# Neighbourhood-attention scores of two heads made together, with the low-part products on half of TensorE's rows each

## The chip, the cores and the metric

The kernel runs on one core of one Trainium2 chip. The metric is the device time of one execution in microseconds (us), as the median of several runs. One further execution was taken by the hardware profiler, and its trace is what is read here.

## What is computed

One layer of a hybrid transformer over 1024 latent tokens (16 rows of a 64-wide grid) with 256 context tokens, width 1024. One input projection feeds a windowed attention (mixer A) and a neighbourhood attention (mixer B), each of 8 query heads of 64 elements. Their outputs are normalised, projected and followed by a SwiGLU feed-forward part (FFN). The change touches the scores of mixer B alone:

```python
def _neighbourhood_latent(q, k, v, k_ctx, v_ctx, rpb):
    ...
    s_loc = jnp.einsum('bnqhd,bnjhd->bnhqj', qb, kg).astype(jnp.float32) * scale + bias
    s_loc = jnp.where(jnp.asarray(mask)[:, None], s_loc, -jnp.inf)
    s_ctx = jnp.einsum('bnqhd,bjhd->bnhqj', qb, k_ctx).astype(jnp.float32) * scale
    p = jax.nn.softmax(jnp.concatenate([s_loc, s_ctx], axis=-1), axis=-1)
    ...
    o = (jnp.einsum('bnhqj,bnjhd->bnqhd', p_loc, vg)
         + jnp.einsum('bnhqj,bjhd->bnqhd', p_ctx, v_ctx))
```

## The kernel before, in words

Products that need more precision than TensorE's one-pass type `F32R` gives are made from two parts: `split` (L117) writes a high part on ScalarE (L119) and the rest, the low part, on VectorE (L122). A head has 64 elements, so the two parts of a head together fill the 128 rows of TensorE.

**Keys of mixer B.** The loop at L357 makes the keys of 128 tokens at a time. `khl` (L366) holds, for each of 8 heads, the high part and then the low part, 64 elements each. It is stored to `kb_d`. `b_kv` (L548) loads it back and transposes it on TensorE, so that `KT[h]` has the head's high part in rows 0 to 63 and its low part in rows 64 to 127, with 1024 local keys and 256 context keys as columns.

**Queries of mixer B.** A step u of the main loop (L893, sixteen of them) is one strip of 16 grid columns (`C`, four) and one pair of heads (`hp_`, four). `b_q` (L568) loads the queries of its two halves (`R`, 8 grid rows each) and two heads, transposes them, and splits them into `QTh` and `QTl`. The store (L535) wrote each query twice, so `QTh[:, j]` has the high part in rows 0 to 63 and again in rows 64 to 127, and `QTl[:, j]` has the low part twice.

**Scores.** `b_front` (L598) calls `scores` (L448) for each half and head, 64 times in all. One call takes a PSUM tile `s` of 1024 columns (the tag has two buffers) and issues four matmuls over all 128 rows at L455: `QTh` against the 256 context keys and the 384 local keys, then `QTl` against the same. So a score is (q high + q low) times (k high + k low). Right behind it VectorE adds the bias and finds the row maximum (`P`, `nm`, L617), ScalarE takes the exponential (L619), and after the four calls of a step GpSimd scales by the reciprocal sum (L625). A `yield` after each call lets `run` put one piece of the step before between two calls.

**The piece of the step before** is `b_back` (L627): four transposes of `P` (L639), a copy out of PSUM (L642 on VectorE, L644 on ScalarE), and products with the values (L652, L656). Those last have 64 columns of weights and write 64 PSUM partitions: head 0 the lower 64, head 1 the upper 64. Their operands are plain f32, and the trace has two instructions for each such `T.matmul`.

**What else runs in these steps.** The output projection of finished tiles: `out_proj` (L809), with TensorE lines L818 to L820 in `F32R`, 512 columns each; and, from u = 10 on, the transposes of `out_b2` (L880). Keys of later head pairs are transposed at L559, queries at L576.

**Order.** The program's order is not the source's. A planner (`schedule_with_timeline_sim=True`, L1385) simulates the kernel when it is built and fixes each engine's order; every engine then executes its list in order. Waits between engines and for buffers are put in by the framework.

Of the kernel before, what the change touches and what calls it, by code (L numbers as in the profile page):

```python
# [7 lines left out]
F32 = mybir.dt.float32  # L8
# [10 lines left out]
HD = 64  # L19
# [37 lines left out]
def f(ap):  # L57
    return ap.bitcast(F32)


def block(tc, d, out, dbg=()):
    nc = tc.nc
    V, S, G, T = nc.vector, nc.scalar, nc.gpsimd, nc.tensor
    load = nc.sync.dma_start

    def pool(name, bufs=1, space=None, side=None):
        kw = {}
        if space is not None:
            kw["space"] = space
        if side is not None:  # L70
            kw["side"] = side
        return tc.alloc_tile_pool(name=name, bufs=bufs, reuse_waits="tile", **kw)
# [44 lines left out]
    def split(hi, lo, src, hi_eng, lo_eng):  # L117
        if hi_eng is S:
            S.activation(hi, src, AF.Copy)  # L119
        else:  # L120
            hi_eng.tensor_copy(hi, src)
        lo_eng.tensor_tensor(lo, src, f(hi), op=ALU.subtract)  # L122
# [118 lines left out]
    def wsplit(wp, nr, nw, c0, n):  # L241
        return [wsplit_k(wp, nr, nw, c0, n, k, V if k % 2 else G) for k in range(8)]
# [11 lines left out]
    def gemm(m, ws, n, tag):  # L254
        pg = gtile(tag)
        for k in range(8):
            gemm_k(pg, m, k, ws[k], n)
        return pg
# [29 lines left out]
    def rope_tables(ipc):  # L288
        ropet = ipc.tile([128, 4, 8, HD], F32, name="ropet")
        load(ropet, d["rope"])  # L290
        gain = ipc.tile([128, 2, HD], F32, name="gain")
        for j, nm in enumerate(("qn_a", "kn_a")):
            load(gain[:, j], d[nm].to_broadcast([128, HD]))
        gsw = ip.tile([128, 512], F32, name="gsw", tag="w1")[:, :2 * HD].rearrange(
            "p (g e) -> p g e", g=2)
        gv = gain[:, 0:2].rearrange("p g (b s q) -> p (g b) s q", b=2, s=2)
        gw = gsw.rearrange("p g (b s q) -> p (g b) s q", b=2, s=2)
        V.tensor_copy(gw[:, :, 0], gv[:, :, 1])
        V.tensor_copy(gw[:, :, 1], gv[:, :, 0])
        for j in range(2):  # L300
            V.tensor_tensor(ropet[:, 2 * j], ropet[:, 2 * j],
                            gain[:, j:j + 1].to_broadcast([128, 8, HD]), op=ALU.mult)
            V.tensor_tensor(ropet[:, 2 * j + 1], ropet[:, 2 * j + 1],
                            gsw[:, j:j + 1].to_broadcast([128, 8, HD]), op=ALU.mult)
        tb.update(ropet=ropet, gain=gain)
# [3 lines left out]
    def store(dst, src, lag=2):  # L309

        waiting.append((dst, src))
        while len(waiting) > lag:
            load(*waiting.pop(0))
# [9 lines left out]
    def headnorm(ps, nh, p):  # L323
        n = nh * HD
        qc = p.tile([128, 512], F32, name="qc", tag="w2")
        S.activation(qc[:, :n], ps, AF.Copy)  # L326
        sq = p.tile([128, 512], F32, name="hsq", tag="w1")
        S.activation(sq[:, :n], qc[:, :n], AF.Square)
        ss = p.tile([128, 32], F32, name="hss")
        V.tensor_reduce(ss[:, :nh], sq[:, :n].rearrange("p (h e) -> p h e", e=HD), axis=AX.X,  # L330
                        op=ALU.add)
        r = rstd_of(p, ss[:, :nh], HD, nh, "hr")
        q3 = qc[:, :n].rearrange("p (h e) -> p h e", e=HD)
        V.tensor_tensor(q3, q3, r.unsqueeze(2).to_broadcast([128, nh, HD]), op=ALU.mult)
        return qc
# [21 lines left out]
    for m in range(10):  # L357
        if m == MV:
            wsv = wsplit(wl, RL, 8, 1792, 512)
        if m == MV + 2:  # L360
            rope_tables(ipc)
        pg = pgs[m] if m < NF else gemm(m, ws, 512, "i")
        qn = headnorm(pg, 8, ip)
        q3 = qn.rearrange("p (h e) -> p h e", e=HD)
        (V if m % 2 else G).tensor_tensor(q3, q3, gkb[:, 0:1].to_broadcast([128, 8, HD]), op=ALU.mult)
        khl = wi.tile([128, 8, 2, HD], F32R, name="khl", bufs=KLB)  # L366
        split(khl[:, :, 0], khl[:, :, 1], q3, S, V)
        store(kb_d[m * 128:(m + 1) * 128], f(khl), LAG)

    def v_b(m, ws, tag):  # L370
# [9 lines left out]
    for m in (8, 9, 0, 1, 2, 3, 4, 5, 6, 7):  # L380
        pg = gemm(m, ws, 256, "i")
        S.activation(Va[:, m].rearrange("p g e -> p (g e)"), pg[:, 128:256], AF.Copy)
        qn = headnorm(pg[:, :128], 2, ip)
# [36 lines left out]
    for m in range(8):  # L420
        pg = gemm(m, ws, 512, "i")
        qn = headnorm(pg, 8, ip)
# [9 lines left out]
    psA = pool("psA", space=PSUM)  # L432
# [15 lines left out]
    def scores(segs, lh, ll):  # L448
        s = psA.tile([128, 1024], F32, name="s", tag="s", bufs=2)
        for n_, l in enumerate((lh, ll)):  # L450
            for o, rhs, n in segs:
                ov = s[:, o:o + n]
                if len(rhs.shape) == 3:
                    ov = ov.rearrange("p (r c) -> p r c", c=rhs.shape[2])
                T.matmul(ov, l, rhs, start=n_ == 0, stop=n_ == 1)  # L455
        return s

    def geo(i):
        b0, b1 = max(i - 1, 0), min(i + 1, 7)
        nl = (b1 - b0 + 1) * 128  # L460
        if i == 7:
            return b0, nl, 512, 256, 256, 0, [8, 9] + list(range(b0, b1 + 1))
        return b0, nl, 512 - nl, 512, 512 - nl, 256 + 384 - nl, list(range(b0, b1 + 1)) + [8, 9]
# [9 lines left out]
    def a_front(i, g, Ps, QT):  # L473
        QTh, QTl = QT
        b0, nl, lo_o, cx_o, s0, m0, blocks = geo(i)
        n = nl + CTX
        nm = at.tile([128, 64], F32, name="nm", bufs=3)[:, :4]
        den = at.tile([128, 64], F32, name="den", bufs=3)[:, :4]
        for h in range(4):
            hh = 4 * g + h  # L480
            s = scores([(lo_o, KTa[:, g, b0 * 128:b0 * 128 + nl], nl),
                        (cx_o, KTa[:, g, SEQ:SEQ + CTX], CTX)],
                       QTh[:, h * 128:(h + 1) * 128], QTl[:, h * 128:(h + 1) * 128])
            P = at.tile([128, 640], F32, name="P", bufs=10)
            V.tensor_tensor_reduce(P[:, :n], s[:, s0:s0 + n], mska[:, m0:m0 + n], -1.0,  # L485
                                   nsink[:, hh:hh + 1], ALU.add, ALU.min, nm[:, h:h + 1])
            S.activation(P[:, :n], P[:, :n], AF.Exp, scale=-1.0, bias=nm[:, h:h + 1],  # L487
                         accum_out=den[:, h:h + 1])
            Ps.append(P)
            yield  # L490
        es = at.tile([128, 128], F32, name="es", bufs=3)[:, :4]
        V.tensor_tensor(es, nm, sink[:, 4 * g:4 * g + 4], op=ALU.add)
        S.activation(es, es, AF.Exp)
        V.tensor_tensor(den, den, es, op=ALU.add)
        V.reciprocal(den, den)  # L495
        for h in range(4):
            G.tensor_scalar(Ps[h][:, :n], Ps[h][:, :n], den[:, h:h + 1], 1.0, ALU.mult, ALU.mult)  # L497
# [100 lines left out]
    def b_front(hp_, C, Ps, QT, bias):  # L598
        QTh, QTl = QT
        KT = kvs[hp_]  # L600
        nm = atb.tile([128, 64], F32, name="nm", bufs=3)[:, :4]
        den = atb.tile([128, 64], F32, name="den", bufs=3)[:, :4]
        for R in range(2):
            r0 = 4 * R
            for h in range(2):
                j = 2 * R + h
                kl = KT[h][:, :SEQ].rearrange("p (r c) -> p r c", c=64)[
                    :, r0:r0 + 12, C0S[C]:C0S[C] + 32]
                kc = KT[h][:, SEQ:]
                if R == 0:  # L610
                    s = scores([(256, kc, 256), (512, kl, 384)], QTh[:, j], QTl[:, j])
                    s0, m0 = 256, 384
                else:
                    s = scores([(128, kl, 384), (512, kc, 256)], QTh[:, j], QTl[:, j])
                    s0, m0 = 128, 0
                P = atb.tile([128, 640], F32, name="P", bufs=PBB)
                V.tensor_tensor_reduce(P, s[:, s0:s0 + 640], bias[h][:, m0:m0 + 640], -1.0,  # L617
                                       3.0e38, ALU.add, ALU.min, nm[:, j:j + 1])
                S.activation(P, P, AF.Exp, scale=-1.0, bias=nm[:, j:j + 1],  # L619
                             accum_out=den[:, j:j + 1])  # L620
                Ps.append(P)
                yield
        V.reciprocal(den, den)  # L623
        for j in range(4):
            G.tensor_scalar(Ps[j], Ps[j], den[:, j:j + 1], 1.0, ALU.mult, ALU.mult)  # L625
# [94 lines left out]
    for u in range(16):  # L720
# [14 lines left out]
        if u == US:  # L735
            psA.release()
            psA = pool("psB", space=PSUM)
# [19 lines left out]
    PsB = []  # L757
    stores_done()
    run(b_front(0, 0, PsB, qtb[0], kin[0][0]), prev)
    o_rstd(0)  # L760
    at.release()
# [389 lines left out]
    for k in range(4):  # L1151
        t = fw.tile([128, 512], F32, name="T3", tag="sg", bufs=SGB)
# [236 lines left out]
```

## Time and profile before

| | us |
|---|---|
| median of 3 runs | 1380.52 |
| lowest and highest | 1379.33, 1381.95 |
| the profiled execution's own time | 1379.55 |
| its span (first to last instruction) | 1377.7 |
| TensorE busy in the span | 1298.1 (94%) |
| VectorE, ScalarE, GpSimd busy | 932.7, 596.0, 621.3 |
| mean granted TensorE clock | 0.984 |

The span begins with loading and projecting the input (to about 210 us), then comes mixer A (to about 436 us), mixer B with the output projection (to about 690 us), and the FFN (to the end). A row "x4" of a timeline stands for four instructions of one kind in a row: the first number is the start of the first, the second is the time from that start to the end of the last. Ends of matmuls overlap the next ones (they are pipelined), so what an instruction costs on TensorE is read from the distance between starts, not from its length. PE is TensorE's matmul, PEld its weight load, DVE VectorE, ACT ScalarE, POOL GpSimd.

### The profile page before, as it was taken

How to read it: one execution, taken by the hardware profiler on the slowest of the kernel's cores; microseconds unless marked ns; L12 is line 12 of the kernel's file. 1: busy time of each engine (PE TensorE's matmuls, PEld its weight loads, DVE VectorE, ACT ScalarE, POOL GpSimd, SP SyncE). 2: the span in 40 equal slices, each digit the busy share in tenths (PEclk: the TensorE clock that was granted, in tenths of full speed). 3: DMA queues.
4: the chain of work that ended last, by engine and by line, in shares of the span. 5: the costliest groups of instructions: out<-in, count | busy, mean ns of one | idle time of the engine just before them, and what ended most of it. 6: DMA issues, size and time to landing. Idle time of an engine off the chain costs nothing. (4 is left out here: it accounts for less than half of the span.)

```text
span 1377.7 us, 18962 instructions
## 1 busy us (share of the span) xinstructions
PE 1298.1 (94%) x6537; PEld 1015.6 (74%) x6537; DVE 932.7 (68%) x1536; ACT 596.0 (43%) x1200; POOL 621.3 (45%) x537
## 2 busy tenths in 40 slices
PE   5989988999998799999979979999999999999998
PEld 3668876777665567777757767888888887888886
DVE  4687676577546465576567887778778765868662
ACT  4555423564445544455546423333333333654440
POOL 1377555442212444575514798676677753000000
PEclk9999999999999899999999999999999999999999
DMA  9735364255317866555373354555554444986732
GB/s 275 227 128 186 100 186 112 69 165 195 117 43 231 223 212 211 203 185 159 116 212 109 105 200 161 178 189 184 191 190 169 169 157 161 393 300 213 259 106 61
DMA packets 185668, 242.85 MB, mean 176 GB/s; under 512 B 44188, under 2 KB 111972, under 8 KB 185444
## 3 DMA queue, kind: packets, MB, share of 16 engines
q1 hardware_dynamic: 185572, 241.65, 54.4%
q8 instruction: 51, 0.84, 0.2%
q14 instruction: 45, 0.37, 0.1%
HBM read 177.91 MB, written 63.70 MB: 175 GB/s over the span
## 5 line engine op out<-in xcount | busy, mean ns | idle before, releaser
L252 PE MATMUL pg<-whi,hl 128*128 128x512 f32 (+1 forms) x368 | 134.1, 375 | 1.9 <-POOL hl L122 1.9
L1222 PE MATMUL pf<-dhl 128*128 128x512 f32 x588 | 134.9, 389 | 0.0
L250 PE MATMUL pg<-whi,hTh 128*128 128x512 f32 (+1 forms) x320 | 122.6, 383 | 7.6 <-ACT qc L326 6.5
L1222 PEld LDWEIGHTS pf<-dhl 128*128 128x128 f32 x588 | 110.4, 188 | 22.9
L122 DVE TENSOR_TENSOR fwhl<-fs,fwhl 128x512 fp32r<-128x512 f32 x88 | 101.2, 1158 | 34.4 <-ACT fwhl L119 31.1
L251 PE MATMUL pg<-wlo,hTh 128*128 128x512 f32 (+1 forms) x320 | 120.8, 378 | 0.0
L497 POOL TENSOR_SCALAR P<-P,den 128x640 f32<-128x640 f32 (+1 forms) x64 | 52.4, 838 | 116.9 <-DVE den L495 78.3
L956 POOL TENSOR_TENSOR fs<-fraw 128x512 f32<-128x512 f32 x44 | 62.9, 1435 | 83.9 <-DMA fraw<-in_w_up_dram 36.4
L119 ACT ACTIVATE fwhl<-fs 128x512 fp32r<-128x512 f32 x88 | 55.1, 627 | 57.9 <-PE pf L997 48.3
L252 PEld LDWEIGHTS pg<-whi,hl 128*128 128x128 f32 x368 | 70.0, 191 | 13.7 <-POOL hl L122 2.6
L122 DVE TENSOR_TENSOR dhl<-draw,dhl 128x512 fp32r<-128x512 f32 x98 | 62.6, 685 | 24.4 <-ACT dhl L119 24.4
L1222 PE MATMUL pf<-fdhl 128*128 128x512 f32 x336 | 78.4, 390 | 0.5 <-DVE fdhl L122 0.4
L119 ACT ACTIVATE dhl<-draw 128x512 fp32r<-128x512 f32 x98 | 55.8, 624 | 52.0 <-PE pf L1222 43.5
L250 PEld LDWEIGHTS pg<-whi,hTh 128*128 128x128 f32 x320 | 61.5, 192 | 20.3 <-ACT qc L326 8.2
L1222 PEld LDWEIGHTS pf<-fdhl 128*128 128x128 f32 x336 | 62.9, 188 | 14.3 <-DVE fdhl L122 1.4
L119 ACT ACTIVATE fwhl<-fraw 128x512 fp32r<-128x512 f32 x54 | 34.1, 632 | 90.3 <-PE pf L997 83.7
L251 PEld LDWEIGHTS pg<-wlo,hTh 128*128 128x128 f32 x320 | 61.7, 193 | 9.0
L625 POOL TENSOR_SCALAR P<-P,den 128x640 f32<-128x640 f32 x64 | 50.6, 811 | 36.9 <-DVE den L623 29.2
L122 DVE TENSOR_TENSOR fwhl<-fraw,fwhl 128x512 fp32r<-128x512 f32 x54 | 66.7, 1234 | 0.4
L487 ACT ACTIVATE P<-P,nm 128x640 f32<-128x640 f32 (+1 forms) x64 | 51.0, 798 | 36.8 <-DVE nm L485 36.8
L485 DVE CUSTOM_DVE_ANT_0 P<-s,mska,nsink 128x640 f32<-128x640 f32 (+1 forms) x64 | 52.4, 845 | 19.4 <-PE s L455 17.2
L619 ACT ACTIVATE P<-P,nm 128x640 f32<-128x640 f32 x64 | 52.7, 824 | 16.3 <-DVE nm L617 16.3
(314 smaller groups left out, 3589.6 us busy)
## 6 DMA issues: line engine op xcount, KB each, us to landing
draw<-f_d SPq DMA_DIRECT2D x35, 512.0 KB
bt<-in_bias_b_dram SPq DMA_DIRECT2D x16, 1024.0 KB
wraw<-in_w_mod_dram SPq DMA_DIRECT2D x48, 256.0 KB
fraw<-in_w_gate_dram SPq DMA_DIRECT2D x22, 512.0 KB
fraw<-in_w_up_dram SPq DMA_DIRECT2D x22, 512.0 KB
wr<-in_w_down_dram SPq DMA_DIRECT2D x22, 512.0 KB
f_d<-sc SPq DMA_DIRECT2D x44, 256.0 KB
t_d<-wt SPq DMA_DIRECT2D x44, 256.0 KB
```

Source lines behind the costliest of these rows:

```text
L119: S.activation(hi, src, AF.Copy)
L122: lo_eng.tensor_tensor(lo, src, f(hi), op=ALU.subtract)
L250: T.matmul(pg[:, :n], l, w[0][:, :n], start=k == 0, stop=False)
L251: T.matmul(pg[:, :n], l, w[1][:, :n], start=False, stop=False)
L252: T.matmul(pg[:, :n], hl[m // 4, k][:, m % 4 * 128:m % 4 * 128 + 128], w[0][:, :n], start=False, stop=k == 7)
L485: V.tensor_tensor_reduce(P[:, :n], s[:, s0:s0 + n], mska[:, m0:m0 + n], -1.0, nsink[:, hh:hh + 1], ALU.add, ALU.min, nm[:, h:h + 1])
L487: S.activation(P[:, :n], P[:, :n], AF.Exp, scale=-1.0, bias=nm[:, h:h + 1], accum_out=den[:, h:h + 1])
L497: G.tensor_scalar(Ps[h][:, :n], Ps[h][:, :n], den[:, h:h + 1], 1.0, ALU.mult, ALU.mult)
L619: S.activation(P, P, AF.Exp, scale=-1.0, bias=nm[:, j:j + 1], accum_out=den[:, j:j + 1])
L625: G.tensor_scalar(Ps[j], Ps[j], den[:, j:j + 1], 1.0, ALU.mult, ALU.mult)
L956: G.tensor_tensor(t, x, y, op=op_)
L1222: T.matmul(pd[t], a[:, x, l], b[:, y], start=start and i == 0, stop=stop and i == 2, skip_group_check=True)
```

## The change

In the keys' tile, every second head has its two parts exchanged: head 0 of a pair keeps the high part in rows 0 to 63, head 1 has it in rows 64 to 127. The queries' high part still meets all 128 rows (k high and k low). The queries' low part meets only the 64 rows with the key's high part, so the product of the two low parts is no longer made. A new `scores2` makes the scores of both heads of a pair: it takes both PSUM tiles, issues the four matmuls of the high parts, and then the four of the low parts, alternating between the heads; those of head 0 use rows 0 to 63 and those of head 1 rows 64 to 127.

```diff
@@ -364,7 +364,9 @@
         q3 = qn.rearrange("p (h e) -> p h e", e=HD)
         (V if m % 2 else G).tensor_tensor(q3, q3, gkb[:, 0:1].to_broadcast([128, 8, HD]), op=ALU.mult)
         khl = wi.tile([128, 8, 2, HD], F32R, name="khl", bufs=KLB)
-        split(khl[:, :, 0], khl[:, :, 1], q3, S, V)
+        kv4 = khl.rearrange("p (u t) a e -> p u (t a) e", t=2)
+        q4 = qn.rearrange("p (u t e) -> p u t e", t=2, e=HD)
+        split(kv4[:, :, 0:4:3], kv4[:, :, 1:3], q4, S, V)
         store(kb_d[m * 128:(m + 1) * 128], f(khl), LAG)
 
     def v_b(m, ws, tag):
@@ -454,6 +456,24 @@
                     ov = ov.rearrange("p (r c) -> p r c", c=rhs.shape[2])
                 T.matmul(ov, l, rhs, start=n_ == 0, stop=n_ == 1)
         return s
+
+    def scores2(segs, lh, ll):
+
+        pair = [psA.tile([128, 1024], F32, name="s", tag="s", bufs=2) for _ in range(2)]
+
+        def view(h, o, rhs, n):
+            ov = pair[h][:, o:o + n]
+            return ov.rearrange("p (r c) -> p r c", c=rhs.shape[2]) if len(rhs.shape) == 3 else ov
+
+        for h in range(2):
+            for o, rhs, n in segs[h]:
+                T.matmul(view(h, o, rhs, n), lh[h], rhs, start=True, stop=False)
+        for x in range(2):
+            for h in range(2):
+                o, rhs, n = segs[h][x]
+                r = slice(64 * h, 64 * h + 64)
+                T.matmul(view(h, o, rhs, n), ll[h][r], rhs[r], start=False, stop=True)
+        return pair
 
     def geo(i):
         b0, b1 = max(i - 1, 0), min(i + 1, 7)
@@ -602,17 +622,17 @@
         den = atb.tile([128, 64], F32, name="den", bufs=3)[:, :4]
         for R in range(2):
             r0 = 4 * R
+            segs = []
             for h in range(2):
-                j = 2 * R + h
                 kl = KT[h][:, :SEQ].rearrange("p (r c) -> p r c", c=64)[
                     :, r0:r0 + 12, C0S[C]:C0S[C] + 32]
                 kc = KT[h][:, SEQ:]
-                if R == 0:
-                    s = scores([(256, kc, 256), (512, kl, 384)], QTh[:, j], QTl[:, j])
-                    s0, m0 = 256, 384
-                else:
-                    s = scores([(128, kl, 384), (512, kc, 256)], QTh[:, j], QTl[:, j])
-                    s0, m0 = 128, 0
+                segs.append([(256, kc, 256), (512, kl, 384)] if R == 0 else [(128, kl, 384), (512, kc, 256)])
+            s0, m0 = ((256, 384), (128, 0))[R]
+            pair = scores2(segs, [QTh[:, 2 * R + h] for h in range(2)], [QTl[:, 2 * R + h] for h in range(2)])
+            for h in range(2):
+                j = 2 * R + h
+                s = pair[h]
                 P = atb.tile([128, 640], F32, name="P", bufs=PBB)
                 V.tensor_tensor_reduce(P, s[:, s0:s0 + 640], bias[h][:, m0:m0 + 640], -1.0,
                                        3.0e38, ALU.add, ALU.min, nm[:, j:j + 1])
```

## Rows read from the trace of the kernel before

**Rows 1.** The page's busy table, share of the span.
```profile
PE 1298.1 (94%) x6537; PEld 1015.6 (74%) x6537; DVE 932.7 (68%) x1536; ACT 596.0 (43%) x1200; POOL 621.3 (45%) x537
```
**Rows 2.** Busy by stretch: A:B, length, PE, PEld, DVE, ACT, POOL; clock, DMA, GB/s.
```profile
436.00:480.00 44.00, 33.66 (x210) 23.25 (x206) 21.10 (x46) 22.10 (x44) 15.83 (x18) 0.93 0.76 207
...
520.00:560.00 40.00, 40.00 (x244) 28.94 (x243) 19.78 (x41) 16.28 (x37) 18.47 (x20) 1.00 0.57 198
```
**Rows 3.** TensorE's timeline from 572.74 to 576.7, without the last scores.
```profile
572.74 0.60 PE L576 MATMUL pt<-ident,qdb 128*128 128x128 f32 x4
573.18 0.60 PE L639 MATMUL pt<-ident,P 128*128 128x128 f32 x4
573.53 0.54 PE L455 MATMUL s<-KTb,QThb 128*128 128x384 f32 x2
573.91 0.46 PE L455 MATMUL s<-KTb,QTlb 128*128 128x384 f32 x2
574.21 0.46 PE L455 MATMUL s<-KTb,QThb 128*128 128x384 f32 x2
574.50 0.46 PE L455 MATMUL s<-KTb,QTlb 128*128 128x384 f32 x2
574.80 0.60 PE L639 MATMUL pt<-ident,P 128*128 128x128 f32 x4
575.33 0.65 PE L652 MATMUL pO<-PT,vp 128*64 128x256 f32 x4
575.91 0.66 PE L639 MATMUL pt<-ident,P 128*128 128x128 f32 x4
576.32 0.54 PE L455 MATMUL s<-KTb,QThb 128*128 128x256 f32 x2
```
**Rows 4.** TensorE's timeline where scores and value products touch.
```profile
631.00 1.08 PE L652 MATMUL pO<-PT,vc 128*64 128x256 f32 x8
632.01 0.57 PE L455 MATMUL s<-KTb,QThb 128*128 128x384 f32 x2
632.42 0.46 PE L455 MATMUL s<-KTb,QTlb 128*128 128x384 f32 x2
632.81 0.66 PE L656 MATMUL pO<-PT,vp 128*64 128x128 f32 x8
633.40 0.56 PE L455 MATMUL s<-KTb,QThb 128*128 128x384 f32 x2
```
**Rows 5.** The chain that ended last: a plain f32 product over the whole array.
```profile
930.49 0.86 PE pf L1045 x2
```
**Rows 6.** The weight loads' timeline at the value products of rows 3; idle time before.
```profile
575.33 0.20 PEld L652 LDWEIGHTS pO<-PT,vp 128*64 128x64 f32 x4 [0.17 <-ACT QThb L119]
575.91 0.42 PEld L639 LDWEIGHTS pt<-ident,P 128*128 128x128 f32 x4 [0.39 <-issue]
```
**Rows 7.** Groups of 436 to 690: busy us, mean ns | idle before, releasers.
```profile
L617 DVE CUSTOM_DVE_ANT_0 P<-s,bt 128x640 f32<-128x640 f32 x64 | 50.8, 819 | 6.2 <-PE s L455 3.2 <-PE pt L639 2.5
...
L455 PEld LDWEIGHTS s<-KTb,QTlb 128*128 128x128 f32 x128 | 22.2, 195 | 0.0
...
L652 PEld LDWEIGHTS pO<-PT,vp 128*64 128x64 f32 x120 | 6.1, 137 | 6.7 <-issue 2.7 <-ACT PT L644 1.1 <-ACT sr L663 0.9
```
**Rows 8.** VectorE's timeline beside the scores of rows 3.
```profile
573.71 1.55 DVE L122 TENSOR_TENSOR ol<-oal,oh 128x512 fp32r<-128x512 f32 x1
575.19 0.81 DVE L617 CUSTOM_DVE_ANT_0 P<-s,bt 128x640 f32<-128x640 f32 x1
```
**Rows 9.** What TensorE waited for from 436 to 720: us, times, longest.
```profile
PE s L455 <- DVE KTb L564: 5.1, 1, 5.1
...
PE s L455 <- DVE nm L617: 1.3, 2, 1.0
```
**Rows 10.** The key tile: ns min/median/max, first and last start.
```profile
L119 ACT ACTIVATE khl<-qc x10: 629/632/633, 77.4 to 135.9; 128x512 fp32r<-128x512 f32 x10
L122 DVE TENSOR_TENSOR khl<-qc,khl x10: 678/692/1783, 80.4 to 137.0; 128x512 fp32r<-128x512 f32 x10
```

## The prediction

> **What bounds the kernel now.** I read the busy table first: TensorE is busy for 94% of the span, the next engine for 68% [rows 1]. Then the busy time by stretch, for mixer B, where the edit lies. From 520 to 560 us TensorE is busy for 40.00 of 40 us, VectorE for half of it; only in the first stretch, 436 to 480, does TensorE stand idle, for 10.3 of 44 us [rows 2], and the waits put half of that down to one wait for the keys and 1.3 us to the score buffers [rows 9]. So from 480 us on TensorE's own list of instructions sets the pace, and a microsecond on it is a microsecond of the kernel, since the output projection stands ready as other work. The last views are the timelines of TensorE and its weight loads, which give what each piece costs from start to start.
>
> **The change, part by part.**
>
> *Low products, removed.* In the timeline one half (R) of a step is eight matmuls: high, low, high, low, two each [rows 3]. The low ones go from 573.91 to 574.21 for one head and from 574.50 to 574.80 for the other: 0.30 + 0.30 = 0.60 us. There are 16 steps with two halves, so 32 such pairs. The high products keep their instructions and weights: no change.
>
> *Low products, added.* The number of low matmuls and their columns stay the same. What is gained is only time in which two run at once. If the heads' halves run abreast, 0.60 becomes 0.30, a gain of 0.30 a pair. The trace of before has no matmul on half of the rows. The nearest rows are the value products, which use half of the columns: head 0 one half, head 1 the other. There eight instructions of 256 columns take 1.01 us (631.00 to 632.01) [rows 4] and four take 0.58 (575.33 to 575.91) [rows 3], so four more cost 0.43. One such f32 instruction over the whole array takes 0.43 us for 512 columns [rows 5], hence about 0.215 for 256 and 0.86 for four, one after another. Four in 0.43 means two abreast, in full. I take that for halves of rows too: 0.30 gained.
>
> *The switch, added.* The same rows show what it costs to leave the full array and come back. Way in: two score matmuls ahead of value products take 0.39 (632.42 to 632.81) where they otherwise take 0.30 [rows 3, 4], and four transposes take 0.53 (574.80 to 575.33) where four ahead of more transposes take 0.44 (572.74 to 573.18) [rows 3]: +0.09 both times. Inside: the first four cost 0.58, the next four 0.43, so 0.15 is fixed. Way out: with scores next, two of them take 0.41 (632.01 to 632.42) in place of 0.30, +0.11 [rows 4]; with transposes next, four take 0.41 (575.91 to 576.32) in place of 0.44, -0.03 [rows 3]. The weight loads show why: they stand idle for 0.17 us before the group and for 0.39 after it, put down to "issue" where no other engine is late [rows 6], while score weights in a stream have no idle time [rows 7]. The array empties, and then a weight load lies open. One round trip is 0.09 + 0.15 - 0.03 = 0.21 with transposes next and 0.09 + 0.15 + 0.11 = 0.35 with one-pass matmuls next. The new group's weights have 128 columns and not 64, and such a load lasts 195 ns against 137 [rows 7]: I add 0.06. So 0.27 or 0.41 a pair.
>
> The array emptying at a change of its division is also what the Trainium skill states (TensorEngine Tiling (Array Packing), Key Properties: "Changing tiling mode (not just tile) drains the TensorE"). It states it of any mode; the rows above agree for halves of columns, and no row here shows halves of rows. By the rule the switch is paid and the gain is eaten up, which speaks against this change.
>
> *Sum on TensorE.* Going through the timeline, 27 of the 32 pairs are followed by transposes or value products, as in rows 3, and five by the output projection. 27 x (0.27 - 0.30) + 5 x (0.41 - 0.30) = -0.8 + 0.55 = -0.26 us. If all were of the one or the other kind: -1.0 or +3.5.
>
> *Making both heads together.* The planner already issues both heads of a pair back to back in most places, as from 573.53 to 574.80 [rows 3], so this moves little on TensorE. But head 0's score is now complete at the end of the pair and not after 0.68 us (573.53 to 574.21), some 0.55 us later. VectorE's L617 waits for it, and behind it on VectorE stand the copies of transposes (L642), the queries' split (L122) and head 1's L617; TensorE's value products and the next use of the score buffer wait for these. Beside the pair at 573.53 this costs nothing: VectorE is busy with the output projection's split until 575.19, past the end of the pair [rows 8]. Over all 64 uses L617 waited 3.2 us for scores [rows 7], so nearly always VectorE was the later one, and the delay is hidden by its backlog. TensorE waited for a score buffer twice, 1.3 us [rows 9]: if each of these grows by 0.55, +1.1. Ends: nothing, or 32 x 0.55 = 17.6 if no delay were hidden anywhere. I take 1.1, since the waits of rows 7 and 9 are few.
>
> *Both buffers at once.* The pair holds both score buffers until its end. Head 1's high matmuls wait for L617 of the pair before, and what stands behind them on TensorE is the planner's choice; it can put output projection there, as it does now. Nothing in steps of 14 us; the rival below prices the rest.
>
> *Keys' layout.* Ten high parts on ScalarE (632 ns) and ten low parts on VectorE (692 ns) at 77 to 137 us [rows 10] write the same elements in other places, 64 or 128 at a stretch. Nothing added, no DMA changed in size: `kb_d` is stored and loaded as before, and no queue is passed. If ScalarE took 10% longer with the wider step, 10 x 0.06 = 0.6 us, beside a projection bound by TensorE. Nothing.
>
> Sum: 1379.55 (profiled execution) - 0.26 + 1.1 = 1380.4. The profiled execution lies 0.97 us below the median of the three runs, so 1381.4 for the median. With the bounds of the switch, and up to five further waits of 0.55: 1379.5 to 1388.
>
> **Rivals.**
>
> *The switch costs nothing on rows (faster).* If the array need not empty between 128 rows and two halves of 64, the gain stays whole: 32 x 0.30 = 9.6 us, 1380.5 - 9.6 + 1.1 = 1372. For it: rows 3 to 6 show the emptying for columns alone. Against it: both are divisions of the same array, and the idle time is put down to "issue", that is to TensorE itself. It decides as soon as a round trip costs under 0.2 us. The skill's page TensorE: Matmul & The Clock Gate (Part 3: Packing small matmuls) gives the span of such a packing as one matmul and some 4 ns for each further tile, with no term for the way in or out; by that the time would be this rival's.
>
> *The halves do not run abreast (slower; the change doesn't do what it says).* If the two halves' matmuls, or their weight loads, go one after another, nothing is gained and the switch is paid: 32 x 0.27 to 0.41 = +8.6 to +13.1, with the 1.1: 1390 to 1395. For it: two row halves both write all 128 PSUM partitions, which the value products do not. Against it: they write different tiles, and rows 3 and 4 show the array doing two things at once.
>
> *The pair waits for its second buffer (slower).* In the last steps the heads are now issued 1.39 us apart (632.01 and 633.40) [rows 4], head 1 after L617 has freed its buffer; this pattern stands at five places from 616 us on. There head 0's softmax would start 1.4 us later. If TensorE has nothing to put in, 5 x 1.4 = +7: 1388. Against it: TensorE has value products in between, and later L617 runs long after its score.
>
> **How the numbers follow.** Forecast (switch and gain cancel) 0.55; no switch cost 0.23; not abreast 0.14; second buffer 0.08. A measurement of this kernel can tell about 0.2%, 2.8 us, from no change. Of the forecast's 0.55, 0.36 lies within that, 0.13 above, 0.06 below. With the rivals: faster 0.06 + 0.21 = 0.27; same 0.36 + 0.02 = 0.38; slower 0.13 + 0.14 + 0.08 = 0.35. The range 1371.5 to 1392 takes in most of both far rivals; its two ends leave out about 0.14. The forecast's own is 1379.5 to 1388.
>
> **What would show it.** In the changed kernel's timeline: four low matmuls of 64 rows in about 0.45 us from the first to the next instruction, starting in twos a few ns apart (against this: starts some 0.12 and 0.18 apart). In the weight loads: idle time put down to issue before and after each low group; if there is none, the first rival holds. In the waits: L617 on scores a few us above 3.2; much more, or TensorE waiting for `nm` L617, is the last rival. The forecast is wrong if the round trip is far from 0.3 us, or if the planner puts other instructions between the two heads' low matmuls, which would pay the switch twice.

## The result and the profile after

| | us | against before, 95% interval |
|---|---|---|
| before, median | 1380.12 | |
| changed kernel, median of 4 | 1396.2 (1394.98 to 1397.0) | 1.0112 (1.0099 to 1.0125) |
| its profiled execution: time, span | 1396.89, 1395.1 | |

The change makes the kernel 16 us slower. The prediction was no change, 1381.4 us, and its range ended at 1392.

The page's busy table of the changed kernel answers to [rows 1]:

```profile
PE 1321.1 (95%) x6537; PEld 1019.5 (73%) x6537; DVE 931.3 (67%) x1536; ACT 597.3 (43%) x1200; POOL 612.3 (44%) x537
```

TensorE is busy for 23 us longer with the same number of instructions; no other engine's busy time grows by more than 4 us. The busy time by stretch answers to [rows 2] (columns as there):

```profile
436.00:480.00 44.00, 35.73 (x204) 23.85 (x202) 19.49 (x44) 20.09 (x39) 13.95 (x16) 0.87 0.69 186
480.00:520.00 40.00, 36.41 (x170) 24.32 (x172) 21.99 (x44) 16.28 (x33) 16.95 (x14) 0.76 0.66 226
520.00:560.00 40.00, 40.00 (x242) 27.68 (x241) 20.10 (x43) 17.10 (x37) 16.57 (x16) 1.00 0.51 173
```

The row that [rows 2] leaves out, of the kernel before:

```profile
480.00:520.00 40.00, 37.61 (x228) 28.53 (x228) 27.49 (x53) 18.99 (x41) 18.04 (x16) 0.94 0.64 220
```

TensorE is about as full as before. Two things differ: the granted clock from 436 to 520 us, 0.87 and 0.76 (0.93 and 0.94 before), and fewer matmuls in the same time. The last row maximum of mixer B (L637) starts at 696.5 us, in the kernel before at 680.3: the whole loss lies in mixer B.

TensorE's timeline of one step of the changed kernel answers to [rows 3] (L470 are the high products, L475 the low ones, L659 the transposes, L672 the value products):

```profile
524.89 0.84 PE L470 MATMUL s<-KTb,QThb 128*128 128x384 f32 x4
525.66 0.56 PE L475 MATMUL s<-KTb,QTlb 64*128 64x384 f32 x4
526.16 0.66 PE L659 MATMUL pt<-ident,P 128*128 128x128 f32 x4
526.74 0.65 PE L672 MATMUL pO<-PT,vp 128*64 128x256 f32 x4
527.33 0.66 PE L659 MATMUL pt<-ident,P 128*128 128x128 f32 x4
527.74 0.54 PE L470 MATMUL s<-KTb,QThb 128*128 128x256 f32 x2
528.21 0.56 PE L475 MATMUL s<-KTb,QTlb 64*128 64x256 f32 x2
528.70 0.56 PE L470 MATMUL s<-KTb,QThb 128*128 128x256 f32 x2
529.18 0.56 PE L475 MATMUL s<-KTb,QTlb 64*128 64x256 f32 x2
529.67 1.09 PE L659 MATMUL pt<-ident,P 128*128 128x128 f32 x8
530.69 0.65 PE L672 MATMUL pO<-PT,vp 128*64 128x256 f32 x4
531.18 0.60 PE L672 MATMUL pO<-PT,vc 128*64 128x256 f32 x4
```

This view holds the case. The first pair is issued as the source has it: four high, then four low. It takes 1.27 us (524.89 to 526.16), the same as before. The second pair was put in another order by the planner: high and low products of head 0, then high and low products of head 1. It takes 1.93 us (527.74 to 529.67), where a pair took 1.28 before: from 576.32 [rows 3] to the transposes in this row of the kernel before.

```profile
577.60 0.60 PE L639 MATMUL pt<-ident,P 128*128 128x128 f32 x4
```

The four low products of the first pair go by in 0.50 us, the two of one head in the second pair in 0.49: two heads run abreast, two products of one head on the same rows don't. Of the 32 pairs, 10 are issued together, one is broken up by transposes, and 21 are issued head by head.

The weight loads' timeline shows the ways in and out, as [rows 6] did:

```profile
525.66 0.30 PEld L475 LDWEIGHTS s<-KTb,QTlb 64*128 64x128 f32 x4 [0.20 <-issue]
526.16 0.42 PEld L659 LDWEIGHTS pt<-ident,P 128*128 128x128 f32 x4 [0.20 <-issue]
...
528.21 0.29 PEld L475 LDWEIGHTS s<-KTb,QTlb 64*128 64x128 f32 x2 [0.19 <-issue]
528.69 0.30 PEld L470 LDWEIGHTS s<-KTb,QThb 128*128 128x128 f32 x2 [0.19 <-DVE QTlb L122]
529.18 0.29 PEld L475 LDWEIGHTS s<-KTb,QTlb 64*128 64x128 f32 x2 [0.19 <-issue]
529.67 0.86 PEld L659 LDWEIGHTS pt<-ident,P 128*128 128x128 f32 x8 [0.19 <-issue]
```

Each row has about 0.2 us without a weight load ahead of it: one such gap at each change between the full array and its halves. Five of the six are put down to "issue". The one put down to VectorE's `QTlb` is as long as the others, and that instruction had ended at 528.45, before the gap began at 528.50. The pair issued together has two, the pair issued head by head four.

### The profile page after: what moved, and what is told of

Read it like the earlier page. It is cut to its first block, busy times and chain, and to the rows that moved or that the text cites. A ratio compares the mean times of both kernels' runs of the same rounds, so it can differ in the third digit from the quotient of the medians.

```text
span 1395.1 us, 18959 instructions
## 1 busy us (share of the span) xinstructions
PE 1321.1 (95%) x6537; PEld 1019.5 (73%) x6537; DVE 931.3 (67%) x1536; ACT 597.3 (43%) x1200; POOL 612.3 (44%) x537
```

## The experiments

Theory A, formed from these rows: a pair issued head by head pays two detours and overlaps nothing, 0.65 us more than before, and 21 of these are the bulk of the loss. Theory B: making both heads together is what costs, since head 0's score and the second score buffer come later. For B speaks the wait of L637 for scores, 10.7 us in the changed kernel (436 to 720 us, all 64 uses) against 3.2 in [rows 7]:

```profile
L637 DVE CUSTOM_DVE_ANT_0 P<-s,bt 128x640 f32<-128x640 f32 x64 | 50.8, 819 | 12.7 <-PE s L475 10.7 <-PE pt L659 0.6 <-issue 0.4
```

| run | median us | ratio to before, 95% |
|---|---|---|
| e2: pair, low parts on full rows | 1379.0 | 0.9988 (0.9977 to 0.9999) |
| e3: half rows, head by head, no pair | 1402.4 | 1.0161 (1.0146 to 1.0176) |
| e4: key layout alone | 1381.3 | 1.0003 (0.9992 to 1.0014) |
| e1: low products kept together, all pairs | 1386.5 | 1.0048 (1.003 to 1.0067) |
| e5: changed kernel from step 4 on | 1387.6 | 1.0052 (1.0037 to 1.0067) |
| e6: changed kernel in steps 0 to 3 alone | 1386.6 | 1.0042 (1.0026 to 1.0058) |
| e7: kept together, from step 4 on | 1381.5 | 1.0000 (0.9986 to 1.0014) |
| e8: kept together, steps 4 to 11 | 1381.4 | 0.9999 (0.9987 to 1.0011) |
| e9: as e8, value products right behind | 1383.6 | 1.0012 (0.9997 to 1.0026) |
| e10: before, value products right behind | 1384.5 | 1.0021 (1.0011 to 1.0031) |

### e2: the same order, no half rows

```diff
-                r = slice(64 * h, 64 * h + 64)
-                T.matmul(view(h, o, rhs, n), ll[h][r], rhs[r], start=False, stop=True)
+                T.matmul(view(h, o, rhs, n), ll[h], rhs, start=False, stop=True)
```

> The changed kernel with the low parts on all 128 rows again (so the product of the two low parts is made again); the order of TensorE's instructions in mixer B is the changed kernel's. Only the division of the array differs. Theory A: no change of division for the scores, so 1379 to 1383 us, the time before. Theory B (pairing costs): the loss stays, 1390 to 1397.

Measured: 1379.0, if anything a little under the kernel before. The pair issued head by head takes 1.28 us (521.03 to 522.31; L470 are the high products, L474 the low ones, L658 the transposes):

```profile
521.03 0.54 PE L470 MATMUL s<-KTb,QThb 128*128 128x256 f32 x2
521.41 0.46 PE L474 MATMUL s<-KTb,QTlb 128*128 128x256 f32 x2
521.71 0.47 PE L470 MATMUL s<-KTb,QThb 128*128 128x256 f32 x2
522.01 0.47 PE L474 MATMUL s<-KTb,QTlb 128*128 128x256 f32 x2
522.31 1.04 PE L658 MATMUL pt<-ident,P 128*128 128x128 f32 x8
```

TensorE's 6537 matmuls stand in the same order as in the changed kernel, from the first to the last. Theory B falls: pairing and its later scores cost nothing. All of the loss, 17 us from e2 to the changed kernel, comes from the division of the array with the order the same.

### e3: half rows with no pair

The kernel before, with the changed layout, and in `scores` (each call passes its head as `half`):

```diff
+                if n_ and half is not None:
+                    r = slice(64 * half, 64 * half + 64)
+                    T.matmul(ov, l[r], rhs[r], start=False, stop=True)
+                    continue
                 T.matmul(ov, l, rhs, start=n_ == 0, stop=n_ == 1)
```

> The kernel before with the changed key layout and the low products on half of the rows, but head by head as before, no pair. All 32 pairs are then issued head by head. Theory A: every pair pays what 21 paid, 32 x 0.65 = 21 us, and the half clock after the wait for the keys stays (about 5 us): 1400 to 1408. Theory B: no pairing, no loss, 1379 to 1385.

Measured: 1402.4, 21.3 us over before: half rows for one head at a time are a pure loss. TensorE's timeline of e3 has the pattern of the second pair above, now in both halves of a step (L461 high, L459 low): 1.94 us from 523.07 to 525.01.

```profile
523.07 0.54 PE L461 MATMUL s<-KTb,QThb 128*128 128x384 f32 x2
523.54 0.55 PE L459 MATMUL s<-KTb,QTlb 64*128 64x384 f32 x2
524.02 0.57 PE L461 MATMUL s<-KTb,QThb 128*128 128x384 f32 x2
524.52 0.56 PE L459 MATMUL s<-KTb,QTlb 64*128 64x384 f32 x2
525.01 0.66 PE L645 MATMUL pt<-ident,P 128*128 128x128 f32 x4
```

### e4: the key layout alone

The kernel before with the three changed lines at `khl`.

> The kernel before with the changed key layout alone (head 1's parts exchanged in the key tile), all products as before. Both theories: the time before, 1379 to 1382; anything over 1385 would mean that the writes of the key tile cost.

Measured: 1.0003. The layout costs nothing.

### e1: the four low products held together

```diff
-                T.matmul(view(h, o, rhs, n), lh[h], rhs, start=True, stop=False)
-        for x in range(2):
-            for h in range(2):
+                high = T.matmul(view(h, o, rhs, n), lh[h], rhs, start=True, stop=False)
+        with tc.issue_after(high.ins):
+            for x in range(2):
+                for h in range(2):
...
```

The three lines below stay as they are, further indented.

> The changed kernel, with one edge more: each low matmul of a pair must be issued behind the last high matmul of the pair, so the four low ones stand together on TensorE in all 32 pairs (in the changed kernel 21 pairs have them head by head, in twos on the same half of the rows). Theory A (a pair issued head by head goes into halves of the array and out again twice and overlaps nothing: 1.93 us from 527.74 to 529.67 where the kernel before took 1.28; 21 pairs x 0.65 = 13.6 us): most of the loss goes; 1380 to 1384 us if the long stretch at half clock (479 to 499 us) goes with it, 1385 to 1389 if that stays. Theory B (making both heads together is what costs, since head 0's row maximum and the second score buffer come later): no better than the changed kernel, 1394 to 1400, since head 0's score is complete later still.

Measured: 1386.5, the most scattered of the runs (1384.13 to 1391.44). Ten of the sixteen us are gone, as A has it, but not all. TensorE's longest waits in e1, by the line that waits and what ended it (total us, count, longest), have this row (L638 is the row maximum):

```profile
PE s L470 <- DVE nm L638: 10.0, 3, 8.9
```

Its timeline of TensorE shows where the longest lies:

```profile
477.23 0.66 PE L660 MATMUL pt<-ident,P 128*128 128x128 f32 x4
486.81 1.65 PE L470 MATMUL s<-KTb,QThb 128*128 128x384 f32 x4 [8.92 <-DVE nm L638]
488.38 0.90 PE L476 MATMUL s<-KTb,QTlb 64*128 64x384 f32 x4
```

In step 2 TensorE stands for 8.9 us at a pair whose score buffer is not free yet. The kernel before stood there for 5.1 us, for the second head's keys [rows 9]. VectorE's timeline shows why the buffer came free so late:

```profile
479.13 0.84 DVE L121 CAST oh<-oal 128x512 fp32r<-128x512 f32 x1 [4.74 <-DMA oal<-oa_d]
485.93 0.81 DVE L638 CUSTOM_DVE_ANT_0 P<-s,bt 128x640 f32<-128x640 f32 x1
```

VectorE's list has splits of other work ahead of the row maximum, and the first of them waits for a DMA until 479.13. So what is left of B is a price for holding pairs together in the first steps, in this order of VectorE's list; pairs alone, in e2, cost nothing there. e7 leaves the first steps out.

### e5, e6, e7: the first four steps apart from the rest

In `b_front`, with `C > 0` for e5 and for e7 (e7 on top of e1), and `C == 0` for e6; the other steps call the kernel before's `scores` (`...` stands for arguments that stay):

```diff
-            pair = scores2(segs, ...)
+            pair = None
+            if C > 0:
+                pair = scores2(segs, ...)
             for h in range(2):
                 j = 2 * R + h
-                s = pair[h]
+                s = pair[h] if pair else scores(segs[h], QTh[:, j], QTl[:, j])
```

> The changed kernel with the kernel before's score calls in the first four steps (C = 0, head by head, all 128 rows) and the pair with half rows from the fifth step on. Of the 24 pairs left, 16 are issued head by head. Theory A1 (0.65 us for each of these, and beside it a longer stretch at half clock that the early half-row products bring after the wait for the keys, 479 to 499 us in the changed kernel against 479 to 485 before, some 5 us): 1380.5 + 16 x 0.65 = 1391 us, with the half clock as short as before. Theory A2 (the clock has no part in it, the pairs alone make the loss): 1396.2 - 5 x 0.65 = 1393, half clock as in the changed kernel.

> The counterpart: the pair with half rows in the first four steps alone, the kernel before's score calls from the fifth on. Theory A1: five pairs head by head, 3.3 us, and some 5 us for the longer half clock: 1388 to 1390. Theory A2: 1383 to 1384.

> The first four steps as in the kernel before; from the fifth on the pair with half rows and all four low products behind the last high one. Both theories of the switch: 24 pairs at 0.49 us for the low group against 0.60 before, less 0.1 for the way in and out, so no change: 1379 to 1382. If the 5 us that the version with all 32 pairs together still lost (1386.5) come from its first steps, where a pair waits for the second head's keys, this one doesn't have them; if they come from the later steps (the second score buffer), it stays at 1384 to 1387.

Measured: e5 is 7.1 us over the median of the kernel before taken beside it (1380.45), e6 6.1; e7 is 1.1 over it by medians, and 1.0000 as a ratio. e7 answers e1: with the first steps left alone, half rows held together are worth nothing that can be measured. Its steps are shorter than before, 14.14 us (519.49 to 533.63) against 14.32 (562.00 to 576.32), but e2, with the full array, has 14.08 (521.03 to 535.11). So the gain lies in the pair's order and not in the half rows.

e5 came out under both expectations: 16 pairs head by head cost 7.1, not 10.4. The pair is 0.65 longer, but the step is not: from the second pair of one step to that of the next it is 14.81 us in the changed kernel (542.55 to 557.36), 0.49 more than before. The timeline above shows the value products of 530.69 and 531.18 side by side, where before each had its own group of transposes ahead of it [rows 3]. e2 has them side by side as well: the order takes 0.24 off the step, and the half rows put 0.73 on it. And in six of e5's sixteen pairs value products stand between the two heads' products; such a pair takes 2.56 us (634.72 to 637.28) against 2.08 before (632.01 to 634.09), 0.48 more and not 0.65.

e6 lies between the two expectations, and its clock is the reason to look at. Busy time by stretch, 484 to 500 us, of the kernel before (columns as in [rows 2]; the clock is the third number from the end):

```profile
484.00:492.00 8.00, 6.27 (x45) 3.53 (x44) 6.88 (x12) 4.64 (x11) 1.05 (x2) 0.97 0.86 288
492.00:500.00 8.00, 7.82 (x43) 6.52 (x44) 3.85 (x9) 2.17 (x5) 4.52 (x6) 1.00 0.56 214
```

The same stretch of the changed kernel:

```profile
484.00:492.00 8.00, 8.00 (x30) 4.80 (x28) 5.65 (x10) 4.06 (x8) 3.41 (x1) 0.50 1.07 323
492.00:500.00 8.00, 7.15 (x36) 4.49 (x34) 2.37 (x6) 2.72 (x7) 3.72 (x5) 0.55 0.61 236
```

Of e2, the same order on the full array:

```profile
484.00:492.00 8.00, 7.66 (x40) 5.31 (x40) 8.00 (x12) 5.58 (x11) 4.57 (x2) 0.76 1.01 320
492.00:500.00 8.00, 7.41 (x50) 5.99 (x51) 3.45 (x11) 3.88 (x9) 3.83 (x5) 1.00 0.74 290
```

And of e6:

```profile
484.00:492.00 8.00, 7.52 (x29) 3.97 (x28) 4.31 (x8) 2.91 (x7) 1.10 (x1) 0.56 1.00 357
492.00:500.00 8.00, 7.55 (x49) 5.82 (x50) 3.38 (x9) 3.73 (x9) 3.82 (x5) 1.00 0.34 121
```

After the wait for keys TensorE's granted clock is at the lower level, 1.2 GHz, in all four. It is back at 2.4 GHz by about 485 us (before), 488 (e2), 491 (e6) and 499 (changed kernel), there with the scores and value products of steps 2 and 3 at half speed. TensorE is no less busy there: 8.00 of 8 us in the changed kernel's first row, with 30 matmuls where the kernel before got through 45. In time of a full clock the changed kernel is short of 16 x (0.985 - 0.525) = 7.4 us from 484 to 500, some of it under idle time.

One stretch of one execution doesn't show that the half rows did this. e8 (below) calls the kernel before's `scores` in these steps, on the full array, and its profiled execution has the lower clock as long as e6:

```profile
484.00:492.00 8.00, 7.59 (x30) 4.34 (x28) 7.60 (x10) 2.70 (x6) 2.04 (x1) 0.53 0.86 277
492.00:500.00 8.00, 7.07 (x51) 5.56 (x50) 4.06 (x11) 4.12 (x9) 3.83 (x5) 1.00 0.72 269
```

There step 4 begins at 507.73 us, 3.2 later than in the kernel before (504.55), and in e6 at 508.08. What speaks for the half rows is the mean granted clock of whole executions, averaged over the runs of a version: 0.976 to 0.980 in the four with half rows in the first steps (changed kernel, e1, e3, e6), 0.981 to 0.983 in the other versions. The two go together; that the one causes the other is not shown.

### e8, e9, e10: looking for a version that beats both

e8 is e7 without the last four steps (`C in (1, 2)`). e9 also holds two groups of transposes of a step behind a group of value products (again with `issue_after`), so that value products follow the low products with no full array between; e10 does that in the kernel before.

> The pair with half rows and the four low products together, in steps 4 to 11 alone (16 pairs); the other steps as in the kernel before. In the run with all steps from the fifth on, head 0's row maximum stood 0.5 us later than before at 503 us, 0.5 us earlier at 615 us, and from there on fell back by up to 3 us, where the heads wait for the second score buffer. Theory (a group of four low products costs some 0.1 us less than the 0.60 of before, way in and out counted, so the grouping gains 0.06 a pair where no buffer is waited for): 1379 to 1380 us, 0.5 to 1.5 under the kernel before. Rival (the gain is chance of the planner's order): within 0.3 us of it or over it.

> As the run of steps 4 to 11, and there two groups of transposes of a step are issued behind a group of value products, so that the value products stand right behind the four low products: from halves of rows to halves of columns, with no full array between. Theory (each way between the full array and a division costs some 0.1 us and an open weight load; here one way in and one way out of two detours fall together): 10 or so places, 0.1 to 0.2 us each, 1 to 2 us under the run of steps 4 to 11: 1377 to 1379. Rival (a change from one division to another empties the array as well, or TensorE waits for the copy of the transposes): no better, 1379 to 1382.

> The kernel before with the same hold on the transposes and no half rows: value products stand right behind the scores. Theory: no way saved, since the scores use the full array; 1380 to 1382. If it gains as much as the run with half rows, the order gives the gain and not the shared change of division.

Measured: e8 0.9999, e9 1.0012, e10 1.0021. No gain, and e9 and e10 came out over what was expected of them. e9 is 0.1% under e10 with the same hold, which fits a saved way in and out, but the intervals overlap, so it is not shown; the hold itself costs e10 0.2%. The gain that e8's expectation read into the middle steps of e7 is better put down to the order of the value products, since e2's steps are as short with no half rows.

## Why the prediction was wrong

- **What bounds the kernel**: right. TensorE's own list decides; e2 and the changed kernel have the same order and differ by 17 us through TensorE alone.
- **Halves of rows run abreast**: right. Four low products of two heads take 0.50 us, two of one head 0.49.
- **The price of the detour**: right in kind, and a little under-sized. 0.27 us was taken; a pair issued together shows 0.35. Its four high products take 0.77 (524.89 to 525.66) against 0.38 + 0.29 in [rows 3]; its four low ones 0.50 against the 0.30 of two abreast; the transposes behind them 0.58 (526.16 to 526.74) against 0.53. That is 0.10 + 0.20 + 0.05. The term that was off is the way out with transposes next, taken at -0.03. Issued head by head, the two detours cost 0.65 within the pair. What was read from halves of columns held for halves of rows, and the rival that the switch costs nothing is out. The Trainium skill states that a change of tiling mode drains the engine (TensorEngine Tiling (Array Packing), Key Properties). The traces agree with it for halves of rows: 0.19 to 0.20 us without a weight load at each change.
- **A pair issued together**: forecast 0.03 us under before, measured 1.27 against 1.28, with 0.05 more in the transposes behind it. e7 gives the same in time: no change.
- **The step that failed** is "The planner already issues both heads back to back in most places ..., so this moves little on TensorE", and with it the count of 32 groups of four. Back to back in the kernel before meant high, low, high, low [rows 3], and the planner kept that order in 21 of 32 pairs. That fits a planner that issues what is ready first; why it did so in these 21 was not tested. So two thirds of the pairs got no overlap and two detours, at 1.93 us where a pair took 1.28. The prediction's last sentence names this as what would make it wrong, and gives it neither a price nor a chance. Its own numbers would have: 21 x (2 x 0.27 + 0.03) = 12.0 us on top of the forecast, some 1393.
- **The later row maximum**: over-sized. 1.1 us was taken. The row maximum did wait longer for scores, 5.8 us in e2, with pairs on the full array, and 10.7 in the changed kernel against 3.2; e2 shows that pairing costs nothing from end to end.
- **The layout**: right, nothing (e4).
- **The rivals**: "the halves do not run abreast" gave 1390 to 1395, near the time measured, but for a reason that doesn't hold: the array does run them abreast, they were not issued so. "The pair waits for its second buffer" was placed in the last steps. In e1 it stands in step 2, 8.9 us long.
- **The clock** was not thought of. The early steps alone cost 6.1 us (e6); five pairs at 0.65 would be 3.3 of it, an estimate.

The two parts, 7.1 (e5) and 6.1 (e6), make 13.2 of the 16 us. The traces show where the rest lies. The first scores of step 4 and of the last pair, in the kernel before and then in the changed one:

```profile
504.55 0.54 PE L455 MATMUL s<-KTb,QThb 128*128 128x256 f32 x2
677.97 0.56 PE L455 MATMUL s<-KTb,QThb 128*128 128x384 f32 x2
```

```profile
512.81 0.54 PE L470 MATMUL s<-KTb,QThb 128*128 128x256 f32 x2
693.82 0.56 PE L470 MATMUL s<-KTb,QThb 128*128 128x384 f32 x2
```

The changed kernel is 8.3 us late at step 4 and 15.9 late at the last pair. So 7.6 us are lost after step 4 begins, about what e5 gives, and 8.3 before it, some 2 more than e6. That goes with the longer stretch at half clock in the full change (to 499 us, in e6 to 491). What makes it last until 491 in one and 499 in the other stays open, and so does how the early loss divides between clock and pairs.

## What to carry to other kernels

Work on part of TensorE's rows pays only if the parts are issued alternately and if what runs abreast is longer than the detour: here 0.30 us a pair was saved against some 0.35 spent, 0.20 of it among the half-row products themselves, 0.10 in the products ahead of them and 0.05 behind. Where a planner sets the order, read its order in the timeline before counting an overlap, and bind the group together: that brought the loss from 16 us to 5 (e1). A comparison run that keeps the order and drops the feature, as e2 does, tells the two apart. A kernel that already switches the array's division should be asked how many switches an edit adds, and not how many columns it saves.

## What the runs showed of the hardware

- Half-row matmuls of two heads start in pairs and take the time of one: in the changed kernel's trace the four low products start at 525.665, 525.668, 525.949 and 525.952. They take 0.50 us for 2 x (384 + 256) columns, against 0.60 on the full array; the product ahead of them and the transposes behind lose 0.15 more. Two on the same half take 0.49.
- Each change between the full array and its halves leaves about 0.2 us without a weight load, 0.19 to 0.20 in all six rows shown.
- After an idle stretch TensorE's clock stayed at 1.2 GHz through dense work: until 499 us in the changed kernel, whose scores there use half rows, and until nearly 492 in e8, whose scores use the full array, where the kernel before was back at 2.4 GHz by 485.
